# Token blocks of 272 and 256 columns, four wide PSUM places for the mixer inputs, and a rounding moved in the MLP

## The chip, the cores and the metric

The kernel runs on one core of a Trainium2 chip, as one program. Its time is the device time of one execution in microseconds (us). Three runs of the kernel before took 2448.08, 2449.39 and 2452.04 us, so 2449.39 us is the median.

## What is computed

The input is 512 tokens of 2048 features, preceded by 16 learned meta tokens, so the sequence has 528 columns. One layer does the following, all in float32:

- `u = rmsnorm(h)`, then `u @ w_in`, which is split into five parts of 2048 columns: `v_pool`, `v_lru`, `v_gelu`, `g_pool` and `g_lru`.
- `v_pool` goes through causal window means of width 2, 4, 8 and 16 (one width for each group of 512 features). The mean minus the token is multiplied by a 512x512 matrix of its group.
- `v_lru` goes through a causal convolution of width 4 and a gated linear recurrence. Its two gates are products with 256x256 matrices, one pair for each of 8 heads, and the recurrence `h_t = a_t h_(t-1) + b_t` runs over the tokens in order of time.
- The two results are gated by sigmoids and a gelu and multiplied by `w_out`. Then comes an MLP with `w1` (2048x8192), a squared ReLU and `w2` (8192x2048), and a last norm. Only the 512 real tokens are returned.

## The kernel before

Activations lie with their features on the 128 partitions and the tokens along the columns. Each float32 product is made from three products of rounded parts: an operand is split into `hi` (rounded) and `lo` (the rest), and `mm3s` issues hi x hi, lo x hi and hi x lo. A weight comes from HBM by SyncE's queue as `raw`. ScalarE writes `whi` from it (line 119) and VectorE writes `wlo` (line 120). In the stages behind the mixer, weights are also added to each other (`sum`, `w2`, line 111), since the products there follow Strassen's scheme with seven products of 256 columns.

The program's first 497 us are the mixer. Here a list of jobs sets the order of the work. A VL or VP job makes one chunk of 128 features of `v_lru` or `v_pool` (16 steps of k, all 528 columns). A GA job makes the gates of one head: four PSUM tiles `ga`, each read by ScalarE into a `gs` (line 483). After these come exp, tanh and sqrt on ScalarE, and VectorE's instructions `n`, `gs` and the scan (lines 499 to 511). After VP, GpSimd adds the shifted windows (`pw`, line 526), VectorE makes the difference `pd` (line 529), and ScalarE and VectorE split it into `a2` (lines 532 and 533). A PW job multiplies four such differences by a group's matrix: four PSUM tiles `ps_pw`, each read by ScalarE into `po` (line 548). An F job writes sums of the inputs for the later stages to HBM through `fx` and `ft` tiles (lines 556 to 576).

The tokens stand as two blocks of 264 columns: 8 meta tokens and 256 real ones in each. A wide PSUM tile holds both blocks, one in each of its two 512-column halves, so what reads it in order of time takes two instructions, one for the meta columns and one for the rest (`PARTS`). Two pools hold the mixer's PSUM tiles: `ps2` has three places of two halves (VL, VP, GA), `ps1` two places of one half (norm, PW).

The instructions of each engine run in the order of the program. A scheduler has put them in that order when the kernel was built, so the order on an engine is not that of the source. An instruction whose input is late holds up everything behind it on its engine.

In the MLP, job j of the first product makes one of 32 chunks, and its sums are stored to HBM (`y_sp`). Later `load_slot` reads them back and `split_slot` splits them, `slot` in lines 898 to 911. The second product takes its moving operands from those slots.

Of the kernel before, what the change touches and what calls it, by code (L numbers as in the profile page):

```python
# [10 lines left out]
F32 = mybir.dt.float32  # L11
# [12 lines left out]
MH = META // 2  # L24
# [6 lines left out]
XW = 576  # L31
JS = 31
# [118 lines left out]
def build(ctx, tc, nc, xt_d, par_d, w_in_d, gate_d, pool_d, woa_d, wob_d, woc_d, w1_d, w2_d, w2t_d,  # L151
# [69 lines left out]
    def ux(k, part):  # L221

        at = (2 * k + part) * XW + 16 * (k // 8)
        return a1[:, at : at + T]
# [120 lines left out]
    with ExitStack() as mx:  # L345
        ps1 = mx.enter_context(tc.tile_pool(name="ps1", bufs=2, space=PSUM))
        ps2 = mx.enter_context(tc.tile_pool(name="ps2", bufs=3, space=PSUM))
# [35 lines left out]
        def psum_v(name):  # L383
            return ps2.tile([P, 2, 512], F32, tag="p2", name=name)

        def products(ts, ws, k):

            s = slice(k % 8 * P, (k % 8 + 1) * P)
            mh, ml = ([ux(k, i)[:, b * TH : (b + 1) * TH] for b in range(2)] for i in range(2))
            for (hi, lo), t in zip(ws, ts):  # L390
                mm3s([t[:, b, :TH] for b in range(2)], (hi[:, s], lo[:, s]), mh, ml, k == 0, k == KD - 1)
# [12 lines left out]
        PARTS = ((slice(0, MH), slice(0, META)), (slice(MH, TH), slice(META, T)))  # L404

        def evac(t, out):

            for s, o in PARTS:
                V.tensor_tensor(blocks(out[:, o]), t[:, :, s], blocks(scale)[:, :, s], op=ALU.mult)

        def raw(t, out):

            for s, o in PARTS:
                S.activation(blocks(out[:, o]), t[:, :, s], AF.Copy)

        def scaled(v):
            for s, o in PARTS:
                V.tensor_tensor(blocks(v[:, o]), blocks(v[:, o]), blocks(scale)[:, :, s], op=ALU.mult)

        xc, xs, pend = {}, {}, []  # L420

        def early(c, t):
            v = keep(f"v{c}")
            V.memset(v[:, :3], 0.0)
            raw(t, v[:, 3:])
# [9 lines left out]
        def job_VR(c):  # L435
# [6 lines left out]
            for i, v in pend:  # L442
                scaled(v[:, 3:])
# [4 lines left out]
        def job_VL(c):  # L448
# [20 lines left out]
        def job_GA(hd):  # L469
            hi, lo = W.next()  # L470
            pt = {}
            for gate in range(2):
                for co in range(2):
                    t = psum_v(f"ga{hd}{gate}{co}")
                    outs = [t[:, h, :TH] for h in range(2)]
                    for ci in range(2):
                        at = gate * 512 + ci * 256 + co * P
                        xh, xl = xs[2 * hd + ci]
                        mm3s(outs, (hi[:, at : at + P], lo[:, at : at + P]),
# [640 lines left out]
```

## Time and profile before

| | us |
|---|---|
| median of three runs | 2449.39 |
| the profiled execution | 2451.99 |
| its span, first to last instruction | 2449.8 |
| TensorE busy | 2383.4 |
| VectorE busy | 1939.2 |
| ScalarE busy | 1222.4 |
| GpSimd busy | 298.1 |

The profile was taken from one execution. Every time below is on its axis, from the start of the span. The engines are PE (TensorE's matmuls), PEld (its weight loads), DVE (VectorE), ACT (ScalarE), POOL (GpSimd) and SP (SyncE). In a timeline a row begins with the start and the time from the first start to the last end of a group of equal instructions; the idle time before it stands in brackets with what ended it. Names of tiles stand without their numbers in the profile, and with them in the order of instructions.

### The profile page before, as it was taken

The numbers are of one execution on the slowest core, as the hardware profiler recorded it, in microseconds if no ns is written. First come the engines' busy times: TensorE is split into PE (matmuls) and PEld (weight loads), VectorE is DVE, ScalarE is ACT, GpSimd is POOL, SyncE is SP. The second block draws the span as 40 slices with busy tenths as digits, with TensorE's granted clock in tenths as the row PEclk, the third lists the DMA queues.
The fourth block names the chain that finished last, engine by engine and source line by source line (L and its number), as shares of the span: only waits on it lengthen the run. The fifth ranks groups of instructions, "written<-read, shape, count | busy, mean of one in ns | idle before, by whom it ended". The sixth has DMA issues, their size and how long they took to land. (4 is left out here: it accounts for less than half of the span.)

```text
span 2449.8 us, 46429 instructions
## 1 busy us (share of the span) xinstructions
PE 2383.4 (97%) x19286; PEld 2327.9 (95%) x19286; DVE 1939.2 (79%) x2444; ACT 1222.4 (50%) x1676; POOL 298.1 (12%) x399
## 2 busy tenths in 40 slices
PE   8999999899999999998899999999989999999997
PEld 8999999899999999887899999999989999999996
DVE  6757766588888886377888888888779888888877
ACT  6644544455555554244444444444455555555445
POOL 0224343300000001032000000000100000000010
PEclk9999999999999999999999999999989999999999
DMA  5245454653444446468454444444566566666553
GB/s 193 87 164 173 167 178 166 244 184 139 146 147 159 155 152 259 158 222 279 137 167 158 154 152 163 166 158 152 203 169 177 175 193 184 189 184 182 151 170 107
DMA packets 119909, 420.33 MB, mean 172 GB/s; under 512 B 13905, under 2 KB 25041, under 8 KB 118033
## 3 DMA queue, kind: packets, MB, share of 16 engines
q1 hardware_dynamic: 78224, 251.82, 30.7%
q0 software_dynamic: 41328, 165.43, 20.8%
q8 instruction: 151, 2.47, 0.4%
q14 instruction: 62, 0.50, 0.1%
q10 hardware_dynamic: 144, 0.10, 0.0%
HBM read 326.21 MB, written 91.10 MB: 170 GB/s over the span
## 5 line engine op out<-in xcount | busy, mean ns | idle before, releaser
L119 ACT ACTIVATE whi<-raw 128x1024 fp32r<-128x1024 f32 (+6 forms) x403 | 402.5, 1003 | 370.8 <-issue 95.6
L120 DVE TENSOR_TENSOR wlo<-raw,whi 128x1024 fp32r<-128x1024 f32 (+6 forms) x403 | 466.1, 1159 | 136.1 <-ACT whi L119 134.7
L119 ACT ACTIVATE whi<-sum 128x1024 fp32r<-128x1024 f32 (+5 forms) x282 | 281.8, 999 | 467.2 <-DVE sum L111 231.4
L120 DVE TENSOR_TENSOR wlo<-sum,whi 128x1024 fp32r<-128x1024 f32 (+5 forms) x282 | 322.5, 1144 | 86.4 <-ACT whi L119 81.0
L342 PE MATMUL ps_A<-a,whi 128*128 128x256 f32 x2048 | 363.0, 280 | 5.0 <-ACT p L621 2.0
L342 PEld LDWEIGHTS ps_A<-a,whi 128*128 128x128 f32 x2048 | 313.8, 190 | 7.2 <-ACT p L621 2.2
L342 PE MATMUL ps_Ab<-a,whi 128*128 128x256 f32 x1728 | 311.5, 280 | 1.2 <-ACT u_b L643 0.6
L342 PE MATMUL ps_A<-a,wlo 128*128 128x256 f32 x1024 | 285.9, 279 | 0.2 <-DVE wlo L120 0.2
L342 PEld LDWEIGHTS ps_Ab<-a,whi 128*128 128x128 f32 x1728 | 264.5, 190 | 2.2 <-ACT u_b L643 1.0
L342 PE MATMUL ps_Ab<-a,wlo 128*128 128x256 f32 x864 | 241.5, 280 | 0.0
L111 DVE TENSOR_TENSOR sum<-sum,raw 128x1024 f32<-128x1024 f32 (+7 forms) x188 | 216.2, 1150 | 5.6
L342 PEld LDWEIGHTS ps_A<-a,wlo 128*128 128x128 f32 x1024 | 194.6, 190 | 0.6 <-DVE wlo L120 0.5
L342 PE MATMUL ps_B<-a,whi 128*128 128x256 f32 x1024 | 180.0, 278 | 2.8 <-DMA a<-gsp_x 2.8
L342 PEld LDWEIGHTS ps_Ab<-a,wlo 128*128 128x128 f32 x864 | 164.0, 190 | 0.2 <-DVE wlo L120 0.2
L342 PEld LDWEIGHTS ps_B<-a,whi 128*128 128x128 f32 x1024 | 155.9, 190 | 3.2 <-issue 3.0
L342 PE MATMUL ps_wo<-a,whi 128*128 128x512 f32 x512 | 158.0, 390 | 0.0
L342 PE MATMUL ps_Bb<-a,whi 128*128 128x256 f32 x864 | 155.3, 279 | 0.0
L337 PE MATMUL ps_vp<-a,whi 128*128 128x264 f32 x896 | 144.7, 283 | 5.6 <-ACT gs L483 5.6
L337 PE MATMUL ps_vl<-a,whi 128*128 128x264 f32 x896 | 144.6, 283 | 1.4 <-ACT gs L483 1.4
L342 PE MATMUL ps_B<-a,wlo 128*128 128x256 f32 x512 | 142.4, 278 | 0.5 <-DVE wlo L120 0.5
L111 DVE TENSOR_TENSOR sum<-w,raw 128x1024 f32<-128x1024 f32 (+7 forms) x94 | 107.3, 1141 | 44.2 <-DMA raw<-w 39.5
L342 PEld LDWEIGHTS ps_Bb<-a,whi 128*128 128x128 f32 x864 | 131.7, 189 | 0.0
(329 smaller groups left out, 5735.9 us busy)
## 6 DMA issues: line engine op xcount, KB each, us to landing
raw<-w SPq DMA_DIRECT2D x168, 512.0 KB, 4.2
raw<-w_in SPq DMA_DIRECT2D x135, 512.0 KB, 3.5
w<-w SPq DMA_DIRECT2D x56, 512.0 KB, 3.7
a<-ysp POOLq DMA_DIRECT2D x27, 896.0 KB, 6.2
hsp<-e POOLq DMA_DIRECT2D x32, 512.0 KB, 6.2
ysp<-t POOLq DMA_DIRECT2D x31, 512.0 KB, 4.4
w<-w_in SPq DMA_DIRECT2D x24, 512.0 KB, 3.8
ysp<-y POOLq DMA_DIRECT2D x31, 384.0 KB, 5.0
```

Of the source, the lines that this page charges most:

```text
L111: nc.vector.tensor_tensor(self.raw[o], self.raw[x], self.raw[y], op=ALU.add)
L119: nc.scalar.activation(hi[:, s], raw[:, s], AF.Copy)
L120: nc.vector.tensor_tensor(lo[:, s], raw[:, s], hi[:, s].bitcast(F32), op=ALU.subtract)
L337: PE.matmul(o, a, r, start=first and i == 0, stop=last and i == 2)
L342: PE.matmul(o, a, b, start=first and i == 0, stop=last and i == 2, skip_group_check=True)
```

## The change

The tokens stay in order of time, 528 columns in a row. They are cut into a block of 272 columns (16 meta tokens and the first 256) and one of 256 (`B0`, `cut`). In a wide PSUM tile of 1024 columns they take columns 240 to 768, so that the cut falls on the border of its halves (`tokens`). What reads such a tile is now one instruction of 528 columns. The start of a moving operand in `ux` changes with it.

The pool `ps1` is gone and `ps2` has four wide places. The norm's two parts and two PW products each now share one wide tile, one in each half. The F job's spills go through five places at the end of `a2` that are taken in turn.

In the MLP, `gaps` between the slots' parts change, so some moving operands start elsewhere. The load of slot 0 is issued at j = 4 in the source, not at j = 30, and its split is tied to a place inside j = 8.

```diff
-        at = (2 * k + part) * XW + 16 * (k // 8)
+        at = (2 * k + part) * XW + (XW - T) * (k < 8)
...
-        ps1 = mx.enter_context(tc.tile_pool(name="ps1", bufs=2, space=PSUM))
-        ps2 = mx.enter_context(tc.tile_pool(name="ps2", bufs=3, space=PSUM))
+        ps2 = mx.enter_context(tc.tile_pool(name="ps2", bufs=4, space=PSUM))
...
+        def psum_v(name):
+            return ps2.tile([P, 1024], F32, tag="p2", name=name)
+
+        def cut(x):
+            return [x[:, :B0], x[:, B0:]]
+
+        def tokens(t):
+
+            return t[:, 512 - B0 : 512 + HS]
+
         def norm1():
+            t = psum_v("psn")
             for h in range(2):
-                t, s = ps1.tile([P, 512], F32, tag="p1", name=f"psn{h}"), slice(h * TH, (h + 1) * TH)
+                s = slice(h * TH, (h + 1) * TH)
                 for i in range(2):
-                    PE.matmul(t[:, :TH], ones, ssq[i][:, s], start=i == 0, stop=i == 1)
-                V.tensor_copy(ssq[0][:, s], t[:, :TH])
+                    PE.matmul(t[:, h * 512 : h * 512 + TH], ones, ssq[i][:, s], start=i == 0, stop=i == 1)
+                V.tensor_copy(ssq[0][:, s], t[:, h * 512 : h * 512 + TH])
             rms_scale(scale, ssq[0], ssq[2], ssq[3])
...
-                mm3s([t[:, b, :TH] for b in range(2)], (hi[:, s], lo[:, s]), mh, ml, k == 0, k == KD - 1)
+                mm3s(cut(tokens(t)), (hi[:, s], lo[:, s]), mh, ml, k == 0, k == KD - 1)
...
-                evac(t, v[:, 3:])
+                V.tensor_tensor(v[:, 3:], tokens(t), scale, op=ALU.mult)
...
-                    S.activation(blocks(s), t[:, :, :TH], AF.Sigmoid,
+                    S.activation(s, tokens(t), AF.Sigmoid,
...
                 if m % 2 == 0:
                     hi, lo = W.next()
-                t = ps1.tile([P, 512], F32, tag="p1", name=f"ps_pw{c}")
+                    both = psum_v(f"ps_pw{c}")
+                t = both[:, m % 2 * SEQ : (m % 2 + 1) * SEQ]
...
-        def spill(t, x, dst, k):
-            put_hl(x, t[:, :HS].bitcast(F32R), t[:, HS:].bitcast(F32R))
-            G.dma_start(dst[:, :, k * HS : (k + 1) * HS], blocks(t))
+        spills = [0]
+
+        def spill(x, dst, k):
+
+            at = 32 * HS + spills[0] % 5 * SEQ
+            spills[0] += 1
+            t = a2[:, at : at + SEQ]
+            put_hl(x, t[:, :HS], t[:, HS:])
+            G.dma_start(dst[:, :, k * HS : (k + 1) * HS], blocks(t.bitcast(F32)))
...
-    gaps = {i: 8 * q for q, i in enumerate((1, 2, 3, 7, 8, 0))}
+    gaps = {1: 16, 2: 40, 3: 16, 7: 40, 8: 16, 0: 40}
...
-        if j == 30:
+        if j == 4:
             load_slot(0, nc.gpsimd)
-        strassen(j, X.get, put, **(dict(head=head, middle=middle) if j == 0 else {}))
-        if j == 30:
-            split_slot(0)
+        strassen(j, X.get, put, **{0: dict(head=head, middle=middle), 8: dict(between=lambda: split_slot(0))}.get(j, {}))
```

The scheduler orders the changed program anew. The last two jobs of the mixer, GA_7 and PW_3, show it. This is VectorE between the rounding of weight 80 and the sums of weights that the next stage needs, before:

```order
L529 SCALAR_TENSOR_TENSOR pd15_5389<-pw15_8_5387,pv15_5378 128x512
L533 TENSOR_TENSOR a2_873<-pd15_5389,a2_873 128x512
L120 TENSOR_TENSOR wlo81_5570<-sum80_5567,whi81_5569 128x1024
L111 TENSOR_TENSOR sum80_5567<-sum80_5567,raw80_5259 128x1024
L499 SCALAR_TENSOR_TENSOR n70_5472<-gs700_5413,e70_5464 128x528
L500 SCALAR_TENSOR_TENSOR n70_5472<-n70_5472,e70_5464 128x528
L499 SCALAR_TENSOR_TENSOR n71_5476<-gs701_5428,e71_5468 128x528
L111 TENSOR_TENSOR sum84_5810<-w2185_5533,raw86_5689 128x1024
```

and after:

```order
L120 TENSOR_TENSOR wlo80_5428<-raw80_5168,whi80_5427 128x1024
L120 TENSOR_TENSOR wlo81_5475<-sum80_5472,whi81_5474 128x1024
L111 TENSOR_TENSOR sum80_5472<-sum80_5472,raw80_5168 128x1024
L111 TENSOR_TENSOR sum84_5714<-w2185_5439,raw86_5593 128x1024
L111 TENSOR_TENSOR w2185_5439<-w2185_5439,raw84_5437 128x1024
L518 SCALAR_TENSOR_TENSOR pd15_5296<-pw15_8_5294,pv15_5286 128x512
L522 TENSOR_TENSOR a2_866<-pd15_5296,a2_866 128x512
```

The names: `pd15` is the last window difference, `a2` its split for PW_3, `sum80`, `sum84` and `w2185` are sums of weights for the next stage, and `raw86` is a weight that SyncE loads into the buffer of `raw80` once `sum80` has been added. The rounding of weight 81 and the sums of weights, which stood behind `pd15`, now stand ahead of it.

This is TensorE in PW_3, with the engines whose semaphores a row waits for, where the fourth product follows the third before:

```order
L337 MATMUL ps_pw14_5538<-a2_873,whi79_5460 128x512 x2
L337 MATMUL ps_pw14_5538<-a2_873,wlo79_5461 128x512
L337 MATMUL ps_pw15_5554<-a2_873,whi79_5460 128x512 [waits Activation_49]
L337 MATMUL ps_pw15_5554<-a2_873,whi79_5460 128x512
L337 MATMUL ps_pw15_5554<-a2_873,wlo79_5461 128x512
L337 MATMUL ps_pw15_5554<-a2_873,whi79_5460 128x512 x2
```

and where the second product follows the third after the change, since each wide tile now carries the names of two products (`ps_pw12` is products 12 and 13, `ps_pw14` is 14 and 15):

```order
L337 MATMUL ps_pw14_5444<-a2_866,whi79_5367 128x512 x2
L337 MATMUL ps_pw14_5444<-a2_866,wlo79_5368 128x512
L337 MATMUL ps_pw12_5399<-a2_866,whi78_5282 128x512 [waits Activation_49]
L337 MATMUL ps_pw12_5399<-a2_866,whi78_5282 128x512
L337 MATMUL ps_pw12_5399<-a2_866,wlo78_5283 128x512
L337 MATMUL ps_pw12_5399<-a2_866,whi78_5282 128x512 x2
```

The products now go 12, 14, 13, 15, and the second product in each tile waits for ScalarE's semaphore, at the value that the reading of the first product in that tile (`po12`, `po14`) brings.

This is ScalarE at the end of PW_3, before:

```order
L548 ACTIVATE po12_5505<-ps_pw12_5492,par_71 128x512
L548 ACTIVATE po13_5535<-ps_pw13_5508,par_71 128x512
L119 ACTIVATE whi82_5626<-sum80_5567 128x1024
L548 ACTIVATE po14_5551<-ps_pw14_5538,par_71 128x512
L119 ACTIVATE whi83_5655<-raw83_5529 128x1024
L548 ACTIVATE po15_5573<-ps_pw15_5554,par_71 128x512
```

and after:

```order
L538 ACTIVATE po12_5412<-ps_pw12_5399,par_71 128x512
L119 ACTIVATE whi82_5530<-sum80_5472 128x1024
L538 ACTIVATE po13_5441<-ps_pw12_5399,par_71 128x512
L538 ACTIVATE po14_5457<-ps_pw14_5444,par_71 128x512
L119 ACTIVATE whi83_5559<-raw83_5435 128x1024
L538 ACTIVATE po15_5478<-ps_pw14_5444,par_71 128x512
```

The rounding of weight 82 has moved ahead of `po13`. It writes into the buffer of weight 78, which products 12 and 13 read.

## Rows read from the trace of the kernel before

**Rows 1.** The page's line of busy time: us, share of the span and number of instructions of each engine.

```profile
PE 2383.4 (97%) x19286; PEld 2327.9 (95%) x19286; DVE 1939.2 (79%) x2444; ACT 1222.4 (50%) x1676; POOL 298.1 (12%) x399
```

**Rows 2.** What TensorE waited for in the mixer, from 60 to 497 us: us in total, times, longest.

```profile
PE ps_pw L337 <- ACT po L548: 9.6, 2, 8.5
PE ps_vp L337 <- ACT gs L483: 5.6, 4, 2.9
PE ps_vl L337 <- ACT gs L483: 1.4, 2, 1.0
PE ga L337 <- ACT gs L483: 1.1, 1, 1.1
PE ga L337 <- DVE pv L409: 0.4, 1, 0.4
PE ga L337 <- DVE v L409: 0.3, 1, 0.3
```

**Rows 3.** ScalarE's timeline in GA_6.

```profile
410.80 0.63 ACT L532 ACTIVATE a<-pd 128x512 fp32r<-128x512 f32 x1 [3.89 <-DVE pd L529]
411.33 1.86 ACT L483 ACTIVATE gs<-ga,par 128x528 f32<-128x528 f32 x3
```

**Rows 4.** VectorE's timeline in GA_7 and PW_3.

```profile
470.16 0.77 DVE L409 TENSOR_TENSOR pv<-ps_vp,scale 128x16 f32<-128x16 f32 x2 [1.23 <-PE ps_vp L337]
471.06 2.10 DVE L120 TENSOR_TENSOR wlo<-raw,whi 128x1024 fp32r<-128x1024 f32 x1
477.90 0.69 DVE L529 SCALAR_TENSOR_TENSOR pd<-pw,pv 128x512 f32<-128x512 f32 x1 [4.75 <-POOL pw L526]
...
482.98 2.20 DVE L111 TENSOR_TENSOR sum<-sum,raw 128x1024 f32<-128x1024 f32 x1
...
491.42 1.23 DVE L111 TENSOR_TENSOR sum<-w,raw 128x1024 f32<-128x1024 f32 x1 [3.50 <-DMA raw<-w_in]
```

**Rows 5.** ScalarE's timeline in GA_7 and PW_3.

```profile
479.17 1.27 ACT L483 ACTIVATE gs<-ga,par 128x528 f32<-128x528 f32 x2
...
482.00 1.28 ACT L493 ACT_TABLE_LOAD   x1
...
488.28 1.18 ACT L502 ACTIVATE gs<-gs 128x528 f32<-128x528 f32 x2
489.37 0.67 ACT L548 ACTIVATE po<-ps_pw,par 128x512 f32<-128x512 f32 x1
```

**Rows 6.** TensorE's timeline in PW_3, and the busy times of a stretch of it. The columns of the last row are us of the stretch, then busy us of PE, PEld, DVE, ACT and POOL with their numbers of instructions, the granted clock, the DMA share and GB/s.

```profile
490.09 1.22 PE L337 MATMUL ps_pw<-a,whi 128*128 128x512 f32 x2 [8.53 <-ACT po L548]
...
496.38 0.63 PE L337 MATMUL ps_pw<-a,whi 128*128 128x512 f32 x2
...
497.08 0.39 PE L342 MATMUL ps_Agl<-a,whi 128*128 128x256 f32 x2
...
486.10:493.00 6.90, 2.91 (x7) 2.33 (x8) 3.37 (x5) 3.90 (x6) 0.61 (x1) 0.51 1.33 347
```

**Rows 7.** VectorE's and TensorE's timelines in PW_1 and F_3.

```profile
252.50 0.72 DVE L556 SCALAR_TENSOR_TENSOR fb<-fb,par,scale 128x512 f32<-128x512 f32 x1
...
255.96 0.41 DVE L572 TENSOR_TENSOR fx<-fb,fx 128x256 fp32r<-128x256 f32 x1
...
254.55 0.66 PE L337 MATMUL ps_vl<-a,whi 128*128 128x264 f32 x4
```

**Rows 8.** TensorE's and ScalarE's timelines at the start of PW_2.

```profile
369.22 0.40 PE L337 MATMUL ps_pw<-a,wlo 128*128 128x512 f32 x1
...
373.67 0.67 ACT L548 ACTIVATE po<-ps_pw,par 128x512 f32<-128x512 f32 x1
```

**Rows 9.** TensorE's timeline at three places, to be read by the distance of the starts: from the first to the second row 24 matmuls of 264 columns, then three of 256 columns in the MLP's first product, and three of 256 columns in its second.

```profile
126.46 0.65 PE L337 MATMUL ps_vl<-a,whi 128*128 128x264 f32 x4
...
129.37 0.64 PE L337 MATMUL ps_vl<-a,whi 128*128 128x264 f32 x4
...
1300.01 0.39 PE L342 MATMUL ps_A<-a,whi 128*128 128x256 f32 x2
...
1300.35 0.39 PE L342 MATMUL ps_A<-a,whi 128*128 128x256 f32 x2
...
1900.23 0.40 PE L342 MATMUL ps_Ab<-a,whi 128*128 128x256 f32 x2
...
1900.59 0.40 PE L342 MATMUL ps_Ab<-a,whi 128*128 128x256 f32 x2
```

**Rows 10.** SyncE's loads of weights: number, KB each, median us from issue to landing; first those that were issued from 466 to 500 us, last those of the whole program, from the page.

```profile
raw<-w_in SPq DMA_DIRECT2D x2, 512.0 KB, 8.5
w<-w_in SPq DMA_DIRECT2D x1, 512.0 KB, 6.6
...
raw<-w_in SPq DMA_DIRECT2D x135, 512.0 KB, 3.5
```

**Rows 11.** The split of slot 0 on ScalarE and VectorE, and the busy times of the stretch behind, columns as in rows 6.

```profile
1195.36 1.49 ACT L910 ACTIVATE slot<-slot 128x1536 fp32r<-128x1536 f32 x1 [10.87 <-DMA slot<-ysp]
...
1196.88 1.76 DVE L911 TENSOR_TENSOR slot<-slot 128x1536 fp32r<-128x1536 f32 x1 [3.59 <-ACT slot L910]
...
1195.00:1206.30 11.30, 8.57 (x46) 7.88 (x46) 9.11 (x11) 6.49 (x10) 1.08 (x2) 0.70 0.45 172
```

More of the change, by code (lines that the diff above doesn't have):

```diff
@@ L23 @@
 HS = SEQ // 2
-MH = META // 2
 KD = D // P
@@ L31 @@
 XW = 576
+B0 = META + HS
 JS = 31
@@ L373, in square_x @@
                 V.tensor_tensor(ssq[k % 2], ssq[k % 2], s, op=ALU.add)
+        def psum_v(name):
[4 more added lines that the diff above has]
+            return t[:, 512 - B0 : 512 + HS]
         def norm1():
+            t = psum_v("psn")
             for h in range(2):
-                t, s = ps1.tile([P, 512], F32, tag="p1", name=f"psn{h}"), slice(h * TH, (h + 1) * TH)
+                s = slice(h * TH, (h + 1) * TH)
                 for i in range(2):
-                    PE.matmul(t[:, :TH], ones, ssq[i][:, s], start=i == 0, stop=i == 1)
-                V.tensor_copy(ssq[0][:, s], t[:, :TH])
+                    PE.matmul(t[:, h * 512 : h * 512 + TH], ones, ssq[i][:, s], start=i == 0, stop=i == 1)
+                V.tensor_copy(ssq[0][:, s], t[:, h * 512 : h * 512 + TH])
             rms_scale(scale, ssq[0], ssq[2], ssq[3])
-        def psum_v(name):
-            return ps2.tile([P, 2, 512], F32, tag="p2", name=name)
         def products(ts, ws, k):
             s = slice(k % 8 * P, (k % 8 + 1) * P)
-            mh, ml = ([ux(k, i)[:, b * TH : (b + 1) * TH] for b in range(2)] for i in range(2))
+            mh, ml = (cut(ux(k, i)) for i in range(2))
             for (hi, lo), t in zip(ws, ts):
-                mm3s([t[:, b, :TH] for b in range(2)], (hi[:, s], lo[:, s]), mh, ml, k == 0, k == KD - 1)
+                mm3s(cut(tokens(t)), (hi[:, s], lo[:, s]), mh, ml, k == 0, k == KD - 1)
         def in_proj(name, n, head=None):
@@ L402, in in_proj @@
             return ts
[L404 to L418, printed above, removed]
         xc, xs, pend = {}, {}, []
@@ L424, in early @@
             V.memset(v[:, :3], 0.0)
-            raw(t, v[:, 3:])
+            S.activation(v[:, 3:], tokens(t), AF.Copy)
             pend.append((c, v))
@@ L442, in job_VR @@
             for i, v in pend:
-                scaled(v[:, 3:])
+                V.tensor_tensor(v[:, 3:], v[:, 3:], scale, op=ALU.mult)
                 conv(i, v)
@@ L474, in job_GA @@
                     t = psum_v(f"ga{hd}{gate}{co}")
-                    outs = [t[:, h, :TH] for h in range(2)]
                     for ci in range(2):
@@ L478, in job_GA @@
                         xh, xl = xs[2 * hd + ci]
-                        mm3s(outs, (hi[:, at : at + P], lo[:, at : at + P]),
-                             [xh[:, h * TH : (h + 1) * TH] for h in range(2)],
-                             [xl[:, h * TH : (h + 1) * TH] for h in range(2)], ci == 0, ci == 1)
+                        mm3s(cut(tokens(t)), (hi[:, at : at + P], lo[:, at : at + P]),
+                             cut(xh), cut(xl), ci == 0, ci == 1)
                     s = tmp(f"gs{hd}{gate}{co}")[:, :T]
-                    S.activation(blocks(s), t[:, :, :TH], AF.Sigmoid,
+                    S.activation(s, tokens(t), AF.Sigmoid,
                                  bias=pv("ab" if gate == 0 else "xb", 2 * hd + co))
@@ L519, in evac_VP @@
             v = tmp(f"pv{c}")[:, :T]
-            evac(t, v)
+            V.tensor_tensor(v, tokens(t), scale, op=ALU.mult)
             w, win = 2 << (c // 4), 1
@@ L554, in job_F @@
             for x, kk in ((a, k), (b, k + 8)):
-                G.dma_start(blocks(x), blocks(xt_d[:, kk])[:, :, MH:])
-                V.scalar_tensor_tensor(blocks(x), blocks(x), pv("g1", kk), blocks(scale)[:, :, MH:],
-                                       op0=ALU.mult, op1=ALU.mult)
+                G.dma_start(x, xt_d[:, kk, META:])
+                V.scalar_tensor_tensor(x, x, pv("g1", kk), scale[:, META:], op0=ALU.mult, op1=ALU.mult)
             (x11, x12), (x21, x22), (t1, t2) = ((x[:, :HS], x[:, HS:]) for x in (a, b, t))
```

10 lines of the change are left out of this document (4 added, 6 removed).

## The prediction

> **What bounds the kernel now.** I read the page's busy times first: TensorE works for 97% of the span, and no other engine for more than 79% [rows 1]. So time can go only where TensorE waits, where it runs at the lower clock, or where one matmul takes longer than it must. Next I read what TensorE waited for in the mixer [rows 2]. Two causes fill the list. The `gs` rows (with `pv` and `v`) belong to GA jobs and sum to 8.8 us. The two `po` rows belong to PW jobs: one wait of 8.5 us and one of 1.1.
>
> The GA waits come from three PSUM places. In GA_6 ScalarE reads the first gate tile, and next in its order is the split of `pd`, for which it stands idle 3.89 us because GpSimd's window sums are late; only then come the other three `gs` in 1.86 us [rows 3]. So the next job finds no free tile. In PW_3 it is the same `pd` that is late [rows 4], and `po` of product 12 comes at 489.37, behind the whole exp, tanh and sqrt chain of GA_7 [rows 5]. TensorE starts again at 490.09 after 8.53 us, at first at half clock: 0.51 of 2.4 GHz from 486.1 to 493.0, that is the 1.2 GHz level [rows 6].
>
> **Fourth place.** After the change a GA job's first tile is free long before the next job wants it, and the three late ones get 11 us or more of other work first. I take the 8.8 us as gone, and with them 0.1 us for each of ten restarts: -9.8. Bounds: -7 and -10.5.
>
> **Shared tiles in PW.** Now two products share a tile, and the order shows that the second waits until ScalarE has read the first. So `po` of the first moves onto TensorE's path, wherever it stands in ScalarE's order. Each job by itself:
>
> PW_0: four matmuls of product 2 (0.93 us) lie between products 0 and 1 and about cover a `po` of 0.67. +0.2.
>
> PW_1: `po4` now stands behind the put of `t3`. VectorE's `fb` starts at 252.50 and takes 0.7; seven instructions of 0.41 follow [rows 7], which overlap a little and take 2.4 to 2.9. So `t3` is made by 255.5, put by 255.9, and `po4` done by 256.6, or 0.5 later. TensorE has its 24 matmuls done at 254.55 [rows 7], 0.5 earlier without GA_3's wait, and four VL matmuls more (0.48): 254.5. A wait of 2.1, in place of the 1.1 of [rows 2]: +1.0.
>
> PW_2: `po8` starts at 373.67 [rows 8]. Ahead of it in ScalarE's order, before and after, stands the convolution's first step, which takes what VectorE has made of the tile of VL_12. One rounding of 1.2 us comes in ahead on VectorE and one of 1.0 goes from ScalarE's chain, so `po8` ends at 374.4 again. TensorE leaves VL_12 at 369.2 [rows 8], or 367.9 without GA_5's wait, and has 17 matmuls of 0.233 to do: 371.9. A new wait of 2.5: +2.5. Bounds for PW_1 and PW_2 together: +1 and +6.
>
> PW_3 is the large one. VP_15 ends at 470.1 [rows 4] and GA_7 is 48 matmuls of 0.121 [rows 9]: 475.9. Behind that end now wait the rounding of weight 81 on both engines (1.06, then about 1.7 on VectorE: between 1.2 free and the 2.10 of [rows 4] beside GpSimd), then `sum80` (1.2): 480.0. Only this frees the buffer for SyncE's load of `raw86`. Such loads took 6.6 and, over two, 8.5 median here [rows 10]; one of the two was the same `raw86`, issued as `sum80` (2.20 from 482.98) ended and landed as the next sum began at 491.42, so 6.2 [rows 4]. I take 6.6: 486.6. VectorE, in order, then does `sum84` and `w2185` (1.2 each) and only then `pd15` (0.65), which was ready to go at 477.9 [rows 4]: 489.7. ScalarE splits it (490.4) and makes three `gs` (1.86, [rows 3]), then tables, exp and tanh (6.28 from 482.00 to 488.28), sqrt 1.1 and `po12` 0.65 [rows 5]: 500.3. Product 13 (12 matmuls of 0.233, 2.8 us) ends at 503.1. The rounding of weight 82 waits for that end, 1.06, then `po13` 0.67 and `po14` 0.67: 505.5. Product 15 ends at 508.3, where before PW_3 ended at 497.1 [rows 6]. +11.2. Of the clock: after 8.5 idle us TensorE had 6.9 us at half. Now it stands idle twice for 6 us or more ahead of product 13; were that at half, +2.8; I take half of it, +1.4. Behind PW_3 the next stage's weights are then early, worth less than 1 us. Bounds of all PW_3: +7 (a load of 3.5, the median of the whole program [rows 10], 3.1 less, at full clock, with the early weights) and +18 (a load of 10.8, the slower of the two behind the 8.5, and both late products at half).
>
> **Blocks of 272 and 256.** A matmul of 264 columns takes 0.121 us by the distance of starts (24 in 2.91); one of 256 takes 0.113 in the first product and 0.120 in the second, where its operand starts elsewhere [rows 9]. No row shows 272. From 264 upward with 8 columns of (0.233 - 0.113) / 256 us I get 0.124 to 0.125. A pair then costs 0.2375 to 0.2445 against 0.241. There are 1728 pairs (16 chunks of VL and of VP with 48 each, 8 heads with 24): -6 to +6 us. With the cheap start in half of them I take -1.
>
> The Trainium skill's page "TensorE: Matmul & The Clock Gate", section "Back-to-back issue gap", makes the distance of matmuls a matter of the columns alone. By it 272 + 256 would be 264 + 264, and this term 0 instead of -1. The trace doesn't agree to that fineness: 256 columns cost 0.113 at one place and 0.120 at another [rows 9].
>
> **Slot 0.** The split of the slot came to stand at j = 2 in ScalarE's order, where its load had not landed: ScalarE was idle 10.87 us, VectorE 3.59 [rows 11]. The stretch behind held 46 matmuls in 11.30 us, which at 0.113 are 5.2: 6.1 lost, half of it by the 1.2 GHz clock that followed (0.70 granted over the stretch). After the change nothing waits there. At j = 8 the load is long there, and 3.4 us of splitting are put on ScalarE and VectorE; VectorE has a fifth of its time free [rows 1] and two products stand ready, so 0 to 2, taken as 0.5. -5.6 in all, bounds -3 and -6.5.
>
> **The small ones.** Reading a tile in one instruction instead of two saves 0.1 us of VectorE, off the path. The norm's second part waits for the copy of the first, with six matmuls between: +0.2. The slots' new starts put some operands of the second product on the slow distance, 112 matmuls net at 0.007: +0.6 to +0.8. The spills' sixth put waits for a DMA, behind `po4` in F_3: 0.
>
> **Sum** on the profiled execution's 2451.99 us: -9.8 + 0.2 + 1.0 + 2.5 + 12.6 - 1.0 - 5.6 + 0.9 = +0.6, less about 0.6 for the next stage's early weights: 0, so 2452. That execution was 2.6 us above the median of the runs shown, so I expect 2449.5 as a median; I say 2449. The gain of GA and slot 0 is paid back in PW_2 and PW_3.
>
> **Rivals.** What a measurement here can tell from no change is about 0.2%, 4.9 us.
>
> Slower: SyncE's load of `raw86` meets the full DMA queues of that moment and takes 10.8 us, and the clock is low for products 13 and 15. It decides from a load of about 9 us on. For it: the median of 8.5 [rows 10]. Against it: the same weight took 6.2. It adds 4.2 for the load and 1.4 to 2.8 for the clock: about 2456. The pace at its bad end would add as much.
>
> Faster by pace: every 256 block runs at 0.113 and 272 at 0.124: 5 more us gone, 2444; with a load of 4 us, 2441. For it: most rows of 256 show 0.113. Against it: two of the four blocks in a pair of steps start where 256 was slow.
>
> Faster without the wait: product 13 follows 14 at once and PW_1 and PW_2 don't wait. Then 14 ends at 493.9, the two products behind it at 499.5 instead of 508.3, and the total is 2449 - 8.8 - 1.4 - 4.6 = 2434. Against it stands the order with its wait, which is in the program. The Trainium skill's page "PSUM — Partial Sum Buffer", section "PSUM bank collisions raise a hardware error", speaks for this rival: engines must be kept apart by bank and quadrant, and two halves of 512 columns are two banks, so this wait is not one that the rule asks for; no run here shows that it could be left out.
>
> The change doesn't do what it says: the GA waits stay, since ScalarE's order behind `pd` is the same. Then 2449 + 9 = 2458. Against it: the order shows each GA job's second tile waiting for old matmuls only.
>
> **Chances.** Forecast 0.52; late load or low clock 0.17; pace or early load 0.20; no waits in PW 0.06; GA waits stay 0.05. With the forecast's own spread of about 4 us this gives faster 0.28, same 0.51, slower 0.21. The likeliest case alone spans 2445 to 2454; the range that leaves out 2 in 10 is 2441 to 2457.
>
> **What would show it.** Right: no `gs` waits of TensorE left; `po` waits of about 2 us in PW_1, 2.5 in PW_2, and in PW_3 waits of about 3 (for the first `gs`), 9, 6 and 2 us; the first matmul of the next stage near 503 (497.1 + 12.6 and less the 6 to 7 gained before it); no `slot` wait on ScalarE near 1195. Wrong: if product 13 starts without `po12`; if `pd15` stands where it stood, near 478; or if TensorE's rows of 272 columns lie above 0.125.

## The result, and the profile after

The changed kernel takes 2455.12 us (median of 11 runs, 2450.83 to 2458.16), the kernel before 2449.68 in the same comparison. The ratio is 1.002 with a 95% interval of 1.0012 to 1.0029: slower by some 5 us, where the forecast was 2449, no change. The time lies inside the range of 2441 to 2457. The profiled execution of the changed kernel took 2455.99 us, 4.0 more than that of before; its span is 2453.9 us.

On the page TensorE is busy as before, for 97% of the span:

```profile
PE 2380.2 (97%) x19286; PEld 2323.5 (95%) x19286; DVE 1938.4 (79%) x2412; ACT 1222.3 (50%) x1673; POOL 288.8 (12%) x399
```

What it waits for in the mixer has changed altogether. The list of TensorE's waits from 60 to 513 us, the whole mixer behind its start (us in total, times, longest us):

```profile
PE ps_pw L337 <- ACT po L538: 11.0, 4, 3.6
PE ps_pw L337 <- ACT a L521: 10.5, 1, 10.5
PE ps_pw L337 <- ACT gs L472: 3.0, 1, 3.0
PE ps_pw L337 <- DVE wlo L120: 1.0, 1, 1.0
```

The GA jobs of [rows 2] are gone from it: no `ga`, `ps_vp` or `ps_vl` row is left. All that is left are PW jobs, 25.5 us together. TensorE's timeline at the seven places where these waits end (the first in PW_1, two in PW_2, four in PW_3), with the row ahead of the first wait and the start of the next stage:

```profile
250.68 0.65 PE L337 MATMUL ps_vl<-a,whi 128*128 128x272 f32 x4
254.94 1.22 PE L337 MATMUL ps_pw<-a,whi 128*128 128x512 f32 x2 [3.61 <-ACT po L538]
...
372.05 0.50 PE L337 MATMUL ps_pw<-a,wlo 128*128 128x512 f32 x1 [1.02 <-DVE wlo L120]
...
375.25 0.73 PE L337 MATMUL ps_pw<-a,whi 128*128 128x512 f32 x2 [2.24 <-ACT po L538]
...
480.47 0.73 PE L337 MATMUL ps_pw<-a,whi 128*128 128x512 f32 x2 [2.97 <-ACT gs L472]
...
493.31 1.52 PE L337 MATMUL ps_pw<-a,whi 128*128 128x512 f32 x2 [10.47 <-ACT a L521]
...
503.13 1.22 PE L337 MATMUL ps_pw<-a,whi 128*128 128x512 f32 x2 [3.27 <-ACT po L538]
...
510.49 0.74 PE L337 MATMUL ps_pw<-a,whi 128*128 128x512 f32 x2 [1.87 <-ACT po L538]
...
513.40 0.40 PE L342 MATMUL ps_Agl<-a,whi 128*128 128x256 f32 x2
```

The last row stood at 497.08 before [rows 6]. The waits are not all. Busy times of two stretches behind such stops, columns as in rows 6, the granted clock behind the five engines:

```profile
254.90:260.50 5.60, 5.56 (x15) 4.42 (x16) 4.56 (x6) 1.62 (x3) 2.54 (x4) 0.53 0.90 272
...
493.00:513.00 20.00, 14.56 (x38) 10.47 (x39) 11.54 (x15) 12.23 (x18) 5.39 (x7) 0.68 0.20 71
```

After the stop of 3.61 us in PW_1 the granted clock is 0.53, the 1.2 GHz level: the first two matmuls of 512 columns behind the stop end 1.22 us after their start, where two take 0.63 at the full clock (before, at 496.38 [rows 6]). In PW_3 the granted clock is 0.68 over 20 us.

Outside the mixer two things went faster. Behind slot 0's old place, over as many us as the last row of [rows 11] (there 46 matmuls in 11.30 us at a clock of 0.70), and in two stretches of the w2 stage, of the kernel after:

```profile
1206.40:1217.70 11.30, 11.30 (x102) 11.30 (x101) 11.24 (x15) 6.89 (x10) 1.08 (x2) 1.00 0.68 237
...
2036.00:2056.00 20.00, 20.00 (x178) 20.00 (x178) 16.21 (x17) 10.95 (x16) 1.41 (x2) 1.00 0.59 173
2056.00:2076.00 20.00, 20.00 (x178) 20.00 (x177) 17.12 (x17) 10.87 (x14) 1.41 (x2) 1.00 0.66 191
```

and the two w2 stretches of the kernel before:

```profile
2036.00:2056.00 20.00, 20.00 (x173) 20.00 (x172) 16.23 (x17) 10.47 (x14) 1.60 (x3) 1.00 0.60 179
2056.00:2076.00 20.00, 20.00 (x172) 20.00 (x171) 16.22 (x16) 10.36 (x14) 1.41 (x2) 1.00 0.61 178
```

With TensorE never idle and the clock at 1.00 in both, 356 matmuls fit into 40 us where 345 did: 112 ns each against 116.

Where the 4 us come from is read by laying the starts of the same matmuls side by side in the two timelines:

| up to | before | after | after minus before | step |
|---|---|---|---|---|
| last matmul of VL_8, ahead of PW_1 | 248.8 | 245.0 | -3.9 | -3.9 |
| last of VP_8, behind PW_1 | 284.5 | 286.0 | +1.4 | PW_1 +5.3 |
| last of VL_12, ahead of PW_2's first wait | 369.1 | 367.5 | -1.6 | -3.1 (-2.6) |
| last of VP_12, behind PW_2 | 403.1 | 407.5 | +4.4 | PW_2 +6.0 (+5.5) |
| last of GA_7 | 479.9 | 477.2 | -2.7 | -7.0 (-2.8) |
| first of the next stage | 497.1 | 513.4 | +16.3 | PW_3 +19.0 (+14.8) |
| first of w1's j = 0 | 1133.2 | 1149.2 | +16.0 | -0.3 |
| last of A at j = 2 | 1216.8 | 1223.5 | +6.7 | slot 0 and j = 0, 1: -9.3 |
| last matmul of w2 | 2434.0 | 2438.2 | +4.1 | w2 -2.6 |

In brackets: before, 18 of PW_3's matmuls (4.2 us at 0.233) ran ahead of GA_7's end, and 2 of PW_2's (0.5 us) inside GA_5, so that much is moved from one row to the next and is no gain or loss. Of the 3.9 us up to VL_8, 0.8 stand ahead of the first GA job. The differences are of unrounded starts.

### The profile page after: what moved, and what is told of

Its sections match the earlier page's. It is cut to its first block, busy times and chain, and to the rows that moved or that the text cites. A ratio compares the mean times of both kernels' runs of the same rounds, so it can differ in the third digit from the quotient of the medians.

```text
span 2453.9 us, 46372 instructions
## 1 busy us (share of the span) xinstructions
PE 2380.2 (97%) x19286; PEld 2323.5 (95%) x19286; DVE 1938.4 (79%) x2412; ACT 1222.3 (50%) x1673; POOL 288.8 (12%) x399
## 5 line engine op out<-in xcount | busy, mean ns | idle before, releaser
L342 PE MATMUL ps_A<-a,wlo 128*128 128x256 f32 x1024 | 284.5, 278 | 0.0
L337 PE MATMUL ps_vl<-a,whi 128*128 128x272 f32 (+1 forms) x896 | 145.9, 284 | 0.0
L337 PE MATMUL ps_vp<-a,whi 128*128 128x272 f32 (+1 forms) x896 | 145.1, 284 | 0.0
```

What stands on the lines that cost most here:

```text
L337: PE.matmul(o, a, r, start=first and i == 0, stop=last and i == 2)
L342: PE.matmul(o, a, b, start=first and i == 0, stop=last and i == 2, skip_group_check=True)
```

## Experiments

All ratios are to the kernel before, from runs on the same chip. Single executions of one kernel lie up to 8 us from its median, so the verdicts rest on medians and the traces tell where the time lies. "The MLP edits" are the move of slot 0 and the new odd places.

**Undoing the places (`three`).** The change with `ps1` (two small places) and three wide ones as before.

```diff
-        ps2 = mx.enter_context(tc.tile_pool(name="ps2", bufs=4, space=PSUM))
+        ps1 = mx.enter_context(tc.tile_pool(name="ps1", bufs=2, space=PSUM))
+        ps2 = mx.enter_context(tc.tile_pool(name="ps2", bufs=3, space=PSUM))
...
-                    both = psum_v(f"ps_pw{c}")
-                t = both[:, m % 2 * SEQ : (m % 2 + 1) * SEQ]
+                t = ps1.tile([P, 512], F32, tag="p1", name=f"ps_pw{c}")
```

> The changed kernel with the places of before: three wide PSUM places for the mixer inputs and two small ones for PW and the norm; blocks of 272 and 256 and the MLP edits stay. By the alignment of the two traces the fourth place gave 11 us in the GA jobs and the shared tiles cost 25 in PW_1, PW_2 and PW_3 (waits and the half clock behind them). Theory 1, the shared tiles are what made the kernel slower: the PW waits go back to about 1 us in PW_1, 0 in PW_2, 8.5 in PW_3, the gs waits come back (about 9 us), and the time is about 2441. Rival, the blocks of 272 and 256 are what cost: the PW stalls or the order around them stay, gs waits come back as well, 2455 to 2466.

2447.37 us, ratio 0.9991 (0.9983 to 1.0). So the four places with shared tiles cost 7.7 us against three places. The `gs` waits are back and PW_2 has no wait. It is not the 14 of the expectation. PW_1 did not go back to the 1 us of before, since two waits for rounded weights (1.6 and 0.6) stand there instead. Most of the 6 us that are missing is the 4.4 by which `three` lies above `mlp_only` (below), these waits among them.

**The MLP edits alone (`mlp_only`) and slot 0 alone (`slot_only`)**, both on the kernel before:

```diff
-    gaps = {i: 8 * q for q, i in enumerate((1, 2, 3, 7, 8, 0))}
+    gaps = {1: 16, 2: 40, 3: 16, 7: 40, 8: 16, 0: 40}
...
-        if j == 30:
+        if j == 4:
             load_slot(0, nc.gpsimd)
-        strassen(j, X.get, put, **(dict(head=head, middle=middle) if j == 0 else {}))
-        if j == 30:
-            split_slot(0)
+        strassen(j, X.get, put, **{0: dict(head=head, middle=middle), 8: dict(between=lambda: split_slot(0))}.get(j, {}))
```

`slot_only` has the second piece without the first.

> The kernel before with only the MLP edits: slot 0 loaded at j = 4 and split at j = 8, and the new odd places. The two traces lie 8.0 us closer together behind the stretch near 1200 us, and 2.5 closer at the end of the w2 stage. Theory, both come from these edits: 2439. By the prediction's terms (-5.6 for the slot, +0.6 to 0.8 for the places): 2445. Rival, the late drift belongs to the run and not to the edit: 2441 to 2442.

> The kernel before with slot 0 loaded at j = 4 and split at j = 8, and the old odd places. By the traces the slot is worth 6 to 8 us and the odd places 2.5 more in the w2 stage: 2443 to 2445 here, with no steps of 0.6 and 0.9 at w2's steps 8, 9, 17, 18, 26 and 27. If the odd places cost 0.6 to 0.8 as the prediction had it: below `mlp_only`, 2442.

`mlp_only` took 2442.95 us (ratio 0.9974, 0.9963 to 0.9986) and `slot_only` 2444.83 (0.9973, 0.9964 to 0.9983). These edits make the kernel 6 to 7 us faster by themselves. The two ratios are alike, so nearly all of it is the slot, and the times can't tell the odd places from nothing. The traces can: in the two w2 stretches above `slot_only` has 172 and 174 matmuls, as before, and `mlp_only` 178 and 178.

**The blocks undone (`places264`)**: the kernel before with the four shared places and the MLP edits, so twice 264 columns. It also has the old order of tokens, the reading of a tile in two instructions and the F job's own tiles for its spills; "the blocks" below are all of these together, and no run takes them apart.

> The change without its blocks: twice 264 columns in the old order of tokens, with the four places, the shared tiles and the MLP edits. `three` lies 4.4 us above `mlp_only` (both have three places; they differ by the blocks), and the traces show 243.2 ns a pair against 240.9. Theory, the blocks cost about 4 us: 2451, and the po waits in PW_1 to PW_3 are there as in the change. Rival, the new blocks brought the order in which the po come late: waits shorter, below 2447. Rival by the prediction's term (-1): 2456.

2452.04 us, ratio 1.0006 (0.9997 to 1.0015), with four `po` waits again (8.6 us, in the change 11.0). Against the change the blocks cost 3.1 us; between `three` and `mlp_only` it is 4.4. They cost; the prediction had -1. The traces show where. The VL and VP jobs each run some 0.06 us longer in the change, 1.7 in all, and from VL_8 to VP_8, across PW_1, it takes 3.5 us longer than `places264` (`three` takes 3.1 longer than `mlp_only`). `places264` shares the tile as well, but the scheduler has put 29 VL matmuls between the first 24 matmuls of PW_1 and the one that waits for `po4`, as in the kernel before, and in the change 4. TensorE waits 1.31 us there, and the clock stays at 1.00 (253 to 259 us).

**The starts of the blocks (`align`)**: the 16 columns more in the second block, and all operands of VL and VP at one start.

```diff
-B0 = META + HS
+B0 = HS
...
-        at = (2 * k + part) * XW + (XW - T) * (k < 8)
+        at = (2 * k + part) * XW
...
-            return t[:, 512 - B0 : 512 + HS]
+            return t[:, 512 - B0 : 512 - B0 + T]
```

> The changed kernel with blocks of 256 and 272 (the 16 columns more in the second block) and every operand of VL and VP at one start of the fast kind (the one where the MLP shows 113.5 ns for 256 columns). In the change a pair of blocks takes 243.2 ns against 240.9 of twice 264, about 3.8 us in the mixer. Theory, the start of the operand sets the distance: 256 columns fall from 118 to 119 to 113.5, 272 stay at 123 to 124, a pair is 237, and about 11 us go: 2444. Rival, something else in the mixer (the length of the matmul ahead, or the place in PSUM) holds 256 columns at 118: pair 242, 2453 to 2455.

2454.92 us, ratio 1.0013 (1.0004 to 1.0022): 0.2 less than the change, and not the 11 of the theory. The pace did change, by less than expected: by the distance of starts in the VL and VP jobs from 152 to 227 us, 256 columns took 0.116 us on average, in the change 0.118, and 272 columns 0.124 in both. So the start of the operand doesn't bring 256 columns to the 0.1135 of the MLP. VP_4 is 96 matmuls in one piece, so its length is the distance from its first row to the first of GA_2, in TensorE's timeline of the kernel before (11.57 us)

```profile
155.02 0.65 PE L337 MATMUL ps_vp<-a,whi 128*128 128x264 f32 x4
...
166.59 0.65 PE L337 MATMUL ga<-xs,whi 128*128 128x264 f32 x4
```

of the change (11.65)

```profile
151.69 0.65 PE L337 MATMUL ps_vp<-a,whi 128*128 128x272 f32 x4
...
163.34 0.65 PE L337 MATMUL ga<-xs,whi 128*128 128x272 f32 x4
```

and of `align` (11.52).

```profile
150.87 0.65 PE L337 MATMUL ps_vp<-a,whi 128*128 128x256 f32 x4
...
162.39 0.65 PE L337 MATMUL ga<-xs,whi 128*128 128x256 f32 x4
```

In the change other VL and VP jobs show 11.60 or 11.66, in `align` all show 11.52. Over 28 such jobs that is about +1.7 us for the change against before, and 3 less for `align`. The 243.2 ns a pair that my expectation speaks of took matmuls beside stalls into its mean, so the 3.8 us in it were too many.

**Both `po` behind the second product (`pairs`)**: the tile stays shared, only the order in the code changes.

```diff
                 if m % 2 == 1:
                     W.advance()
-                z = tmp(f"po{c}")[:, :SEQ]
-                S.activation(z, t, AF.Copy, scale=pv("ps", c))
-                G.dma_start(pl_sp[c % 8][:, c // 8, :], z)
+                    for i in (c - 1, c):
+                        z = tmp(f"po{i}")[:, :SEQ]
+                        S.activation(z, both[:, i % 2 * SEQ : (i % 2 + 1) * SEQ], AF.Copy, scale=pv("ps", i))
+                        G.dma_start(pl_sp[i % 8][:, i // 8, :], z)
```

> The changed kernel with the two po of a shared tile emitted behind the second product, so that no product waits for the reading of the other half; four places as in the change. Theory 1 (the wait on the shared tile): TensorE has no po wait in PW_1, PW_2 or PW_3 any more, the clock stays at 2.4 GHz in PW_1 and mostly in PW_2, the wait for the split of pd in PW_3 (10.5) stays since VectorE's order is the same there, and about 16 us go: 2439. Rival, the wait only moves: the tile is held longer, the next job finds no free place, and gs or po waits of the same length stand at VL_9, VL_13 and the next GA: above 2450. Rival, the stalls are covered elsewhere: 2455.

2447.82 us, ratio 0.9988 (0.9979 to 0.9996): 7.3 less than the change, under half of what I expected. TensorE's waits of `pairs`, 60 to 560 us:

```profile
PE ps_pw L337 <- ACT a L521: 9.0, 1, 9.0
PE ps_Agl L342 <- ACT p_gl L617: 4.8, 1, 4.8
PE ps_pw L337 <- ACT gs L472: 3.0, 1, 3.0
PE ga L337 <- ACT xs L457: 2.0, 2, 1.3
...
```

No `po` wait is left, but two new ones stand there: GA_4 and GA_5 now wait for `xs` (2.5 us with VectorE's part), and the next stage waits 4.8 us for `p_gl`. ScalarE's timeline of `pairs` tells what `p_gl` waits for:

```profile
509.68 0.38 ACT L617 ACTIVATE p_gl<-ps_Agl 128x256 f32<-128x256 f32 x1 [3.37 <-DMA lr<-xc]
```

It is the DMA that stores GA_7's result: its memory has to be free for the next stage. GA_7's `gs` stand behind the split of `pd15` on ScalarE, so a late `pd15` delays this store too.

**The same for PW_0 to PW_2 alone (`pairs012`) and for PW_3 alone (`pairs3`)**, with the condition `g < 3` or `g == 3` on the edit of `pairs`.

> The changed kernel with the two po behind the second product in PW_0, PW_1 and PW_2 only; PW_3 as in the change. The prediction charged the shared tiles in PW_0 to PW_2 with 3.7 us (bounds 1 to 6 for PW_1 and PW_2); the alignment of the traces shows 5.3 and 6.0 in PW_1 and PW_2, of which 4 are half clock behind the stops. Theory, those two jobs are the mis-sized term: TensorE's stops there go, some 2.5 us come back as waits for xs ahead of GA_4 and GA_5 as in `pairs`, and 7 to 9 go: 2446 to 2448. By the prediction's term: 2451 to 2452. Rival, what TensorE gains there is late again in PW_3: 2455.

> The changed kernel with the two po behind the second product in PW_3 only. The po waits of 3.3 and 1.9 in PW_3 and the half clock around them go, some 9 us; but in `pairs`, where PW_3 ended as early, TensorE then stood 4.8 us at p_gl and the half clock went on. Theory, in PW_3 the wait for pd and the next stage's weights set the end: 1 to 4 us go, 2451 to 2454, and `pairs012` and `pairs3` together give what `pairs` gave (7.3). Rival, PW_3's po waits are the main cost: 2446 to 2448.

`pairs012` took 2447.58 us (ratio 0.999, 0.9978 to 1.0001) and `pairs3` 2454.81 (1.002, 1.001 to 1.0029). So PW_0 to PW_2 alone give 7.5, no less than the 7.3 of `pairs`, and mending PW_3's order of `po` alone gives 0.3, nothing that the medians can tell from zero. Laid beside the trace of the change, `pairs012` takes 6.4 us less in PW_1 and 5.3 less in PW_2, and 2.3 of them are lost again in GA_4 and GA_5. `pairs3` ends PW_3 8.7 us earlier, and 6.6 of these are lost again by the first matmul of w1. In TensorE's waits of `pairs3`, 60 to 560 us, the next stage waits for `p_gl` again:

```profile
...
PE ps_Agl L342 <- ACT p_gl L618: 4.2, 1, 4.2
...
```

**`pd15` ahead of the sums: `after_pd`, `pairs_pd`, `mlp_pd`.** One edge keeps what the planner issues on VectorE at the end of GA_7 behind the split of `pd15`:

```diff
-            V.tensor_tensor(lo, d, hi.bitcast(F32), op=ALU.subtract)
+            last[0] = V.tensor_tensor(lo, d, hi.bitcast(F32), op=ALU.subtract)
...
-            W.advance()
+            if hd == 7:
+                with tc.issue_after(last[0].ins):
+                    W.advance()
+            else:
+                W.advance()
```

`after_pd` is the change with this edge, `pairs_pd` is `pairs` with it, `mlp_pd` is `mlp_only` with it.

> The changed kernel with only the edge that puts the planner's roundings and sums at the end of GA_7 behind the split of pd15; the tiles stay shared and each po stands behind its own product. Theory, two separate causes: the wait for pd15 (10.5 in the change) goes, the po waits of PW_1, PW_2 and PW_3 stay, and the time is `pairs_pd` plus what pairs gave without the edge (7.3): 2442. Rival, the po waits of PW_3 grow by what the pd wait gives free, since po12 stands behind the exp, tanh and sqrt of GA_7 in ScalarE's order: 2448 or more. Rival, the edge does it all: 2435.

> The run `pairs` with one edge more: what the weights' planner issues on VectorE at the end of GA_7 (three roundings and the sums behind them) comes behind the split of the last pd, so that no instruction that waits for the load of raw86 stands ahead of pd15. Theory 1, VectorE's order ahead of pd15 made PW_3's wait of 9.0 to 10.5: that wait falls under 2 us, PW_3 ends 8 to 9 us earlier, and about 2440. Rival, the same load bounds the next stage: in `pairs` TensorE waited 4.8 us for p_gl, behind roundings that need raw86; then PW_3 ends earlier, the wait at gl grows by as much, and the time stays at 2446 to 2449.

> The kernel before with the MLP edits and the edge on pd15; three wide places, twice 264 columns, nothing shared. In the kernel before pd15 already stands ahead of the sum that waits for raw86. Theory, the edge mends an order that only the change brought, and the gs waits and the 8.5 us for po12 stay: 2442 to 2443, as `mlp_only`. Rival, the edge helps any version (roundings out of the way of pd): 2435.

In this order they took 2446.28 us (0.9982, 0.9973 to 0.9991), 2434.72 (0.9933, 0.992 to 0.9946) and 2443.94 (0.9973, 0.9962 to 0.9984). `after_pd` is 4 slower than its theory and `pairs_pd` 5 faster: the two causes are not separate. The edge takes 8.8 us from the change, 13.1 from `pairs` and none from `mlp_only`. Together with `pairs` it takes 20.4, more than 7.3 and 8.8: each alone leaves one of two things that hold TensorE at the end of the mixer. The change's VectorE around `pd15`:

```profile
480.48 1.23 DVE L111 TENSOR_TENSOR sum<-sum,raw 128x1024 f32<-128x1024 f32 x1
489.50 1.23 DVE L111 TENSOR_TENSOR sum<-w,raw 128x1024 f32<-128x1024 f32 x1 [7.80 <-DMA raw<-w_in]
490.76 1.23 DVE L111 TENSOR_TENSOR w<-w,raw 128x1024 f32<-128x1024 f32 x1
491.90 0.68 DVE L518 SCALAR_TENSOR_TENSOR pd<-pw,pv 128x512 f32<-128x512 f32 x1
```

The load of `raw86` is issued when the first of these sums has been added, in SyncE's timeline:

```profile
481.77 0.33 SPq L96 DMA_DIRECT2D raw<-w_in  x1
```

`pd15` stands fourth on VectorE, behind the sum that is idle for 7.80 us while this load is under way (7.7 us from issue to the start of that sum). In `pairs_pd`:

```profile
468.76 0.69 DVE L522 SCALAR_TENSOR_TENSOR pd<-pw,pv 128x512 f32<-128x512 f32 x1 [6.55 <-POOL pw L519]
...
484.59 1.23 DVE L111 TENSOR_TENSOR sum<-w,raw 128x1024 f32<-128x1024 f32 x1 [3.50 <-DMA raw<-w_in]
```

Now `pd15` waits only for GpSimd's window sums, and the load lies beside PW_3. TensorE's waits of `pairs_pd`, 60 to 560 us:

```profile
PE ps_Cgl L342 <- DVE wlo L120: 4.5, 1, 4.5
PE ps_pw L337 <- ACT gs L472: 3.0, 1, 3.0
PE ps_Agl L342 <- ACT p_gl L623: 1.3, 1, 1.3
```

8.8 us, where the change has 25.5. In the same view of `after_pd` the wait for `pd` is gone and the `po` waits stay, about as long as in the change (11.0):

```profile
PE ps_pw L337 <- ACT po L544: 11.6, 4, 4.0
PE ps_pw L337 <- ACT gs L472: 3.0, 1, 3.0
...
```

**Looking for more: `pairs264`, `pairs264_pd`, `align_pd`.** `pairs` with twice 264 columns, the same with the edge, and `pairs_pd` with the edits of `align`.

> Twice 264 columns, four places, the two po of a shared tile behind the second product, and the MLP edits. If the parts add up: `pairs` less 4.4 for the blocks, 2443, no better than the MLP edits alone with three places (2443), since the next stage waits for its weights. If the fourth place is worth more than that with the old blocks, 2436 to 2440.

> Four places with the two po behind the second product, twice 264 columns, the MLP edits and the edge on pd15. If the blocks of 272 and 256 cost 3 to 4 us here too: `pairs_pd` less that, 2431. If waits for weights take it back: 2435.

> `pairs_pd` with the blocks and starts of `align` (256 and 272, every operand of VL and VP at one start). In the trace of `align` a pair of VL or VP took 240.1 ns against 243.2 in the change, 4.7 us over 1536 pairs, while its median fell by 0.2 only. If the pace counts now that the waits are gone: 2430 to 2431. If what TensorE gains there is late elsewhere: 2434 to 2435.

In this order they took 2444.18 us (0.9974, 0.9963 to 0.9986), 2435.49 (0.9936, 0.9924 to 0.9948) and 2434.58 (0.9938, 0.9927 to 0.995). `pairs264` gained the 3.6 that the blocks cost elsewhere; once the edge is in, neither the blocks nor the starts move the time. With the old blocks the wait for the next stage's weight is longer (4.5 in `pairs_pd`), first in the list of TensorE's waits of `pairs264_pd`, 60 to 560 us:

```profile
PE ps_Cgl L342 <- DVE wlo L120: 7.1, 1, 7.1
...
```

The best version is `pairs_pd`, with `align_pd` and `pairs264_pd` not to be told from it: 15 to 16 us faster than before, 20 faster than the change.

## Why the prediction was wrong

| term | forecast | traces |
|---|---|---|
| fourth place, GA jobs | -9.8 | -11 (10.3 of stops, the rest restarts) |
| PW_1 | +1.0 | +5.3 |
| PW_2 | +2.5 | +5.5 |
| PW_3, with the clock | +12.6 | +14.8 |
| next stage's early weights | -0.6 | -0.3 |
| blocks of 272 and 256 | -1.0 | +1.7 |
| slot 0 | -5.6 | -8.0 |
| odd places, norm, PW_0 | +1.1 | about -2 |

The last column sums to +6.0 and the traces lie 4.1 apart; the rest, -1.9, stands at the start of the mixer and in w1's j = 0 and 1, where single executions of one kernel differ by as much. That the sum is only 4 us off is luck: PW_1, PW_2, PW_3 and the blocks cost 12.5 us more than I had, and the fourth place, slot 0, the odd places and the rest gave back 8.6. The clearest sign is the first matmul of the next stage, which I had near 503 and which came at 513.4. (The sum as I wrote it comes to +0.8 and not +0.6, which changes nothing.)

**The step that failed is PW_1 and PW_2**, "PW_1 and PW_2 together: +1 and +6" in its bounds: the traces show 10.8. The mechanism was right, the second product of a shared tile waits for the first one's `po`. Its size was off for three reasons.

First, TensorE came to PW_1 earlier than I had it. I took off GA_3's wait alone (0.5). But the gains of all GA jobs ahead add up: the lead is 3.9 us by VL_8 in the table, most of it from them. `po4` hangs on `t3`, near the end of VectorE's job F_3, and came only 1.7 us earlier than I had it. Its job's `fb` began at 250.79 and not at 252.50 [rows 7], and the way from there to the end of `po4` took 4.1 us, as I had it (VectorE's and ScalarE's timelines of the change):

```profile
250.79 0.73 DVE L546 SCALAR_TENSOR_TENSOR fb<-fb,par,scale 128x512 f32<-128x512 f32 x1
...
254.22 0.67 ACT L538 ACTIVATE po<-ps_pw,par 128x512 f32<-128x512 f32 x1
```

TensorE was done at 251.3 (250.68 and 0.65) and not at 254.5. So the stop was 3.61 us, not 2.1, and part of the fourth place's gain was given back there at once. The rows of before showed that `po4`'s time is set by VectorE [rows 7], which the fourth place hurries by less than half as much as TensorE; what has to be laid against it is TensorE's whole lead. In PW_2 this played no part, since the lead had been spent: TensorE left VL_12 at 367.6, where I had it at 367.9, and the `po` wait was 2.24 us, where I had 2.5.

Second, the clock. I priced the half clock behind PW_3's long stops only. In PW_1 it stood at 0.53 for 5.6 us behind a stop of 3.61, in which 15 matmuls ran; that alone is some 2.5 of the 5.3, and in PW_2 about 1.6 of the 5.5 (by the products that started 0.43 us apart and not 0.233). It is not of this one execution only: in the traces of `after_pd`, `pairs3` and `align`, which go the same way through both jobs, the low clock costs 1.5 to 1.8 us in each of them.

Third, in PW_2 TensorE waited 1.02 us for a rounded weight ahead of the `po` wait, which I didn't see coming.

That a shared tile need not cost so much in PW_1 is shown by `places264`: with 29 VL matmuls ahead of the waiting product and not 4, the wait is 1.31 us and the clock stays up.

`pairs012` shows that these two jobs are the cause: with their `po` out of the way 7.5 us go in the medians, though 1.3 us of waits for `xs` come up, and 6.4 and 5.3 in the traces of the two jobs. By my terms it would have been 3.7.

**PW_3 was right in kind and short by 2.** The four stops were forecast as about 3, 9, 6 and 2 and measured as 2.97, 10.47, 3.27 and 1.87. The chain that I worked out (rounding of weight 81, `sum80`, the load of `raw86`, `sum84`, `w2185`, then `pd15`) is the one in VectorE's rows above; only the load took 7.7 and not 6.6. The low clock cost about 4 us more than before and not 1.4: 20 products started 0.43 us apart, before 5 did. That the wait for `pd15` is caused by this order, and not by the load as such, is shown by the edge.

**What PW_3 hides** I had not thought of. Its `po` waits look like 5 us and are worth 0.3 in the medians (`pairs3`), since the next stage's `p_gl` waits for the store of GA_7, and that hangs on `pd15` as well. The prediction's rival "faster without the wait" (2434) assumed that product 13 could follow at once and the next stage begin at once; without the edge the second half of that is false.

**The blocks** had the wrong sign. The 272 columns took 0.124 us, as I had it. I assumed the cheap 0.113 for half of the 256 blocks, and they took 0.118 on average. In one piece, VP_4 shows 11.65 us against 11.57. That is 1.7 over the mixer, while the medians put the blocks at 3.1, 3.6 and 4.4 in three pairs of kernels and at -0.8 in the fourth. In two of these pairs (`places264` and the change, `mlp_only` and `three`) the traces have the rest in PW_1, by the order told above. In a third (`pairs264` and `pairs`) PW_1 has no stop, and what the rest is there was not found; that nothing is left of it when the mixer's end is mended fits work that is hidden at the wait for the next stage's weight, where `pairs264_pd` stands 7.1 us and `pairs_pd` 4.5, but is not shown by it. The formula of the Trainium skill's page "TensorE: Matmul & The Clock Gate", section "Back-to-back issue gap", in which columns alone count, does not hold to this fineness: 96 matmuls of 25,344 columns in all took 11.52, 11.57, 11.60 or 11.66 us.

**The slot** was worth 8.0 instead of 5.6 in the traces (of the 9.3 in the table of starts, 8.0 fall at the slot's old place, in j = 2), 5.7 in the medians (`slot_only` against the 2450.58 of before beside it). I had both the wait and the lost clock; nothing of the splitting at j = 8 shows, where I had charged 0.5. **The odd places** were forecast as a loss of 0.6 to 0.8, because I counted operands moved to a slow start; in the w2 stage more matmuls are quick (178 in 20 us and not 172 or 173).

The time came out near the "slower" rival's 2456, but not by its mechanism: that asked for a load of 10.8 us, and the load took 7.7; its other half, the low clock, did happen. That the two numbers are close is luck. Of the rival without waits, the other rule of the Trainium skill that I had weighed, on its page "PSUM — Partial Sum Buffer", section "PSUM bank collisions raise a hardware error", stays untried: `pairs` takes the wait away by order, and no run here lets TensorE write one half of a tile while ScalarE reads the other.

## What to carry to other kernels

When a change lets one engine run ahead, carry its whole lead along to the next thing that it waits for, and look whether that thing hurries as well; if not, the lead is spent there, and here the low clock behind the stop cost 1.5 to 2.5 us more. When two results share a buffer whose waits go by the whole buffer, emit both readers behind both writers. And in an engine that works in order, an instruction that waits for a load must not stand ahead of one that the critical path wants; the price is the rest of the load and everything that hangs on the late one, here up to the next stage.

## What the runs showed of the hardware

The same stop does not always cost the same clock. The mixer of `mlp_only` and of `slot_only` is that of the kernel before, in the same order on every engine, and in all three TensorE stops behind GA_6 for a `gs` (2.87 us in each). The busy times of the stretch behind it, of the kernel before:

```profile
411.90:418.00 6.10, 5.93 (x49) 5.93 (x50) 1.15 (x3) 6.07 (x10) 2.62 (x2) 1.00 0.00 0
```

of `mlp_only`:

```profile
413.30:419.50 6.20, 5.90 (x27) 5.90 (x28) 1.25 (x3) 6.17 (x10) 2.58 (x2) 0.50 0.00 0
```

and of `slot_only`:

```profile
411.20:417.00 5.80, 5.66 (x34) 5.66 (x35) 0.89 (x2) 5.77 (x10) 2.60 (x2) 0.71 0.00 0
```

The granted clock is 1.00, 0.50 and 0.71, and the stretches hold 49, 27 and 34 matmuls: behind one stop of 2.87 us TensorE lost nothing, 2.7 and 1.5 us in three executions. Once a shorter stop was enough: behind GA_4, TensorE stopped for 1.86 us in `mlp_only`, and 14 matmuls of 264 columns behind it started 0.22 us apart and not 0.12, which cost 1.5 us; behind the stop of 1.54 us at that place in the kernel before none did. In the change the stop of 2.97 us ahead of PW_3 left the clock alone (1.00 from 480.4 to 482.8 us), and the one of 3.27 us inside PW_3 did not (0.50 from 503.0 to 508.0). So a stop of this length has to be priced with anything from nothing to nearly its own length again, and one trace doesn't tell which.
